# A delta-rule chunk chain on 64-row by 64-column quarters of the array, and a padded LoRA product

## The chip, the cores and the metric

The kernel runs on one core of one Trainium2 chip. A core has TensorE (PE, matmuls into PSUM banks), VectorE (DVE), ScalarE (ACT), GpSimdE (POOL) and SyncE (SP, which issues most DMAs). The metric is device time in microseconds of one execution; lower is better. The kernel before was run three times: 1617.15, 1622.96 and 1626.52 us, median 1622.96 us.

A matmul `mm(out, lhsT, rhs)` computes `lhsT.T @ rhs`. `lhsT` is loaded into the array as the stationary operand (the trace shows this as PEld), `rhs` is streamed through it. Slices of 64 partitions use 64 rows of the array, and the partitions of `out` decide which columns of the array are used. In the trace's rows "64\*64 64x64" means 64 rows by 64 columns of the array, and an output of 64 partitions by 64 elements. A float32 matmul stands in the trace as two records, a float32r matmul as one.

## The reference, cut to what matters

The block has differential attention and an RWKV-7 branch; both are merged, projected and followed by a feed-forward part. The change touches the RWKV-7 branch only:

```python
w = -jax.nn.softplus(-(w0 + jnp.tanh(wd) @ w2)) - 0.5     # LoRA of the decay
a = jax.nn.sigmoid(a0 + ad @ a2)                          # LoRA of a
def step(state, inp):                                     # 1024 steps, 8 heads of 64x64 state
    r_t, w_t, k_t, v_t, a_t, b_t = inp
    sa = jnp.einsum('bhvk,bhk->bhv', state, a_t)
    state = (state * w_t[:, :, None, :] + sa[..., None] * b_t[:, :, None, :]
             + v_t[..., None] * k_t[:, :, None, :])
    return state, jnp.einsum('bhvk,bhk->bhv', state, r_t)
```

Everything is computed in float32 accuracy: a float32 operand of a projection is split into a high and a low float32r part, and three of the four products are added (`mm3`).

## The kernel before, in words

**Stages.** `rwkv_parallel` projects the inputs and does all of the RWKV-7 branch that needs no state: for each pair of heads (4) and each 256 tokens (4) one `rwkv_unit`, with two calls of `lora_mm` (L395). These 32 calls stand between the projections' 128x512 matmuls, in an order that the scheduler chose. `lora_mm` makes two products of 256 columns: `lw2h` or `la2h`, the high weights, on 128 rows (the high part of x on partitions 0 to 63, its low part on 64 to 127), and `lw2l` or `la2l`, the low weights, on 64 rows, with the high part of x alone.

Then attention, the inversion of small triangular matrices, the gate projections (`gates`, L1059) and the state recurrence (`chain`, L917) run together. From there on TensorE's order is written out by hand: each part is a generator that yields the time from which its next piece can go on, and `drive` (L1488) takes the ready one of the lowest rank. The clock of this plan, `self.now`, is not the chip's: `mm` adds a fixed cost for each matmul (0.214 us for a float32 matmul with 128 stationary columns, 0.07 us with 64). So a cost in `mm` decides how many gate matmuls (`ps_d<-h_hi,whi` and its like) stand between two steps of the chain. After the chain, `branch_a` goes on with the same filling, then merge, output projection and feed-forward, all of 128x512 matmuls.

**The chain.** It has 16 chunks of 64 tokens, and in each the 8 heads as 4 pairs. A pair's two heads stand on partitions 0 to 63 and 64 to 127. `Sb` (state), `Ub` (corrections) and `Vb` (values) are block-diagonal, 128 x 4 x 128, with zeros off the diagonal, so that one 128x128 product handles both heads. One chunk takes three stretches of matmuls, with other work between:

1. `AK` @ `Vb` (4 products, 128 rows by 128 columns), `KT` @ `Vb` (8 products, 64 by 64, one for each head on the diagonal quarters), `AR` @ `Sb` (4 products, 128 by 128). ACT and DVE copy the upper half of the result to `R`.
2. `T` @ `R` (8 products, 64 by 64). ACT and DVE copy it to `Ub`.
3. `BT` @ `Ub` (8 products, 64 by 64), then `RB` @ `Ub` (4 products, 128 rows by 64 columns). DVE adds the first to `W` (the decayed state, from POOL) to give the next `Sb`; ACT copies the second to `yn`, from which the group norm starts.

Bank `g` holds AK, AR and RB; bank `us` holds T in one half and KT with BT in the other. After stretch 1 the chain yields for `LH1` (2.106 us), after 2 for `LH2` (1.8 us), after 3 for `LH` (2.215 us). In the trace the tile names `ps_r<-Vb,ch`, `ps_r<-Sb,ch`, `ps_r<-R,cT` and `ps_r<-Ub,ch` are AK with KT, AR, T, and BT with RB. In the first chunk there is no AR, in the last no KT and no BT.

Of the kernel before, what the change touches and what calls it, by code (L numbers as in the profile page):

```python
# [81 lines left out]
class Block:  # L82
# [102 lines left out]
    def mm(self, out, lhsT, rhs, **k):  # L185
        self.pe(self.nc.tensor.matmul(out, lhsT=lhsT, rhs=rhs, **k))  # L186
        if rhs.dtype == F32R:
            self.now += max(0.06, rhs.free_size() * 0.000417)
        else:
            self.now += {P: 0.214, C: 0.07}.get(lhsT.free_size(), 0.04)  # L190
# [165 lines left out]
    def loras(self):  # L356
# [7 lines left out]
        for src, nm in ((self.lw2, "lw2"), (self.la2, "la2")):  # L364
# [4 lines left out]
            lo = p.tile([C, HB], F32R, name=nm + "l")  # L369
            nc.scalar.copy(hi, raw)  # L370
            nc.vector.tensor_tensor(lo, raw[0:C], f32(hi[0:C]), ALU.subtract)
# [23 lines left out]
    def lora_mm(self, which, pr, u, tag):  # L395
# [7 lines left out]
        self.mm(ps, lhsT=wl[:, cs], rhs=x[0:C], start=False, stop=True)  # L403
# [513 lines left out]
    def chain(self):  # L917
# [7 lines left out]
        def zeroed(nm):  # L925
            t = p.tile([P, 4, P], F32, name=nm)
            nc.gpsimd.memset(t, 0.0)
            return t

# [5 lines left out]
        Sb, Ub, Vb = zeroed("Sb"), zeroed("Ub"), (zeroed("Vb0"), zeroed("Vb1"))  # L935
        lds = {}

        def load(c):
# [5 lines left out]
            for h in range(2):  # L944
                nc.sync.dma_start(Vb[c % 2][H[h], :, H[h]], self.d_vt[c, H[h]])
# [9 lines left out]
        for c in range(NC_):  # L955
# [3 lines left out]
            ld, Vc = lds.pop(c), Vb[c % 2]  # L959
            T = ld["T"]  # L960
            R = p.tile([P, 4, C], F32, tag="R", name="R")

            g = self.pst("r").rearrange("p (r x) -> p r x", x=P)
            us = self.pst("r").rearrange("p (z r x) -> p z r x", z=2, x=C)
            for pr in range(4):
                mm(g[:, pr, :], lhsT=ld["AK"][:, pr, :], rhs=Vc[:, pr, :], start=pr == 0, stop=False, skip_group_check=True)
            if not last:
                for pr in range(4):
                    for h in range(2):
                        mm(us[H[h], 1, pr, :], lhsT=ld["KT"][H[h], pr, :], rhs=Vc[H[h], pr, H[h]], start=pr == 0, stop=False, skip_group_check=True)  # L970
            if not first:
                for pr in range(4):
                    mm(g[:, pr, :], lhsT=ld["AR"][:, pr, :], rhs=Sb[:, pr, :], start=False, stop=False, skip_group_check=True)
            with self.hi_first():
                nc.scalar.copy(R[H[0]], g[H[0], :, H[0]])
                V.tensor_copy(R[H[1]], g[H[0], :, H[1]])
            yield self.now + LH1
            for pr in range(4):
                for h in range(2):
# [642 lines left out]
```

## Time and profile before

| what | value |
|---|---|
| median of three runs | 1622.96 us |
| the profiled execution's own time | 1619.49 us |
| its span, first to last instruction | 1617.7 us |
| PE busy | 1573.7 us, 97% of the span |
| DVE busy | 1114.6 us, 69% |
| ACT busy | 760.9 us, 47% |
| mean granted TensorE clock | 0.993 |

The busy time of PE is modelled and overlaps from one matmul to the next, so what a matmul costs is read as the time from its start to the start of the next one. In the rows of the timeline a group of equal matmuls has its first start and its count; the cost of a group is the next row's start less its own.

### The profile page before, as it was taken

Reading aid. Unit: us, or ns where it says so; the run is one execution under the profiler, and the core shown is the slowest. Engines: PE = TensorE matmul, PEld = TensorE weight load, DVE = VectorE, ACT = ScalarE, POOL = GpSimd, SP = SyncE. Lnnn points to the kernel's source line nnn. Section 1 sums busy time; section 2 is a strip of 40 time slices with the busy share of each in tenths; the row PEclk is TensorE's granted clock in tenths of the full one; section 3 lists DMA queues with packets and bytes.
Section 4 is the critical chain, followed back from the end, with each engine's and each line's share of the span. In section 5 each row is a group of like instructions: output and inputs, shape, how many; then the busy total and the mean of one; then the engine's idle time right before and its main releaser. Section 6 shows DMA issues by size and latency. Waiting matters only on the chain.

```text
span 1617.7 us, 24697 instructions
## 1 busy us (share of the span) xinstructions
PE 1573.7 (97%) x8786; PEld 1305.9 (81%) x8786; DVE 1114.6 (69%) x2201; ACT 760.9 (47%) x1509; POOL 141.6 (9%) x337
## 2 busy tenths in 40 slices
PE   9999999989999999999999999999999999999997
PEld 7888878868777887787877888888888888888887
DVE  7657677776596576767358678766676557977646
ACT  6533434443445554554334455444445454554423
POOL 2100000000011233323330000000000000000000
PEclk9999999999999999999999999999999999999999
DMA  5224445455769765563674553555555578554403
GB/s 185 92 69 148 136 138 145 143 157 173 237 207 254 213 190 174 176 193 119 232 244 144 201 180 133 195 170 177 193 171 171 180 237 282 170 157 137 137 27 105
DMA packets 217997, 274.63 MB, mean 170 GB/s; under 512 B 89617, under 2 KB 125586, under 8 KB 217618
## 3 DMA queue, kind: packets, MB, share of 16 engines
q1 hardware_dynamic: 208946, 251.46, 49.7%
q0 software_dynamic: 3456, 12.58, 2.5%
q10 hardware_dynamic: 5472, 9.02, 1.5%
q8 instruction: 69, 1.13, 0.3%
q14 instruction: 54, 0.44, 0.1%
HBM read 178.10 MB, written 94.90 MB: 169 GB/s over the span
## 4 chain that ended last, share of the span: by engine, by line
PE 84%; DVE 6%; DMA 6%; issue 1%; ACT 1%; POOL 1%; SPq 0%; ACTq 0%; DVEq 0%; POOLq 0%
PE ps_d L186 22%; PE ps_e L186 19%; PE ps_r L186 19%; PE ps_t L186 14%; PE ps_s L186 9%; PE ps_t L193 2%; DMA sin<-in_sin_dram 1%; DMA x_in<-in_xT_dram 1%; DMA q_s<-d_q 1%; DMA d_ch<-AR 1%; DMA bv<-d_bv 1%; DMA y_in<-d_yb 0%; DMA tb<-d_gt 0%; DVE sm L841 0%; DMA lraw<-in_la_dram 0%
## 5 line engine op out<-in xcount | busy, mean ns | idle before, releaser
L201 ACT CAST whi<-wraw 128x1024 fp32r<-128x1024 f32 (+1 forms) x122 | 114.1, 937 | 152.5 <-PE ps_d L186 53.6
L202 DVE TENSOR_TENSOR wlo<-wraw,whi 128x1024 fp32r<-128x1024 f32 (+1 forms) x122 | 133.5, 1094 | 37.3 <-ACT whi L201 37.0
L186 PE MATMUL ps_d<-h_hi,whi 128*128 128x512 f32 x344 | 141.5, 411 | 3.6 <-DVE rope L692 1.9
L186 PE MATMUL ps_d<-h_hi,wlo 128*128 128x512 f32 x344 | 137.5, 400 | 0.0
L186 PE MATMUL ps_d<-h_lo,whi 128*128 128x512 f32 x344 | 137.0, 398 | 0.1
L201 ACT CAST wop<-wop 128x512 fp32r<-128x512 f32 x98 | 60.9, 621 | 105.8 <-DMA wop<-d_z 103.4
L202 DVE TENSOR_TENSOR wop<-wop 128x512 fp32r<-128x512 f32 x98 | 67.3, 687 | 56.2 <-ACT wop L201 56.0
L186 PE MATMUL ps_e<-h_hi,whi 128*128 128x512 f32 x256 | 102.0, 398 | 0.0
L186 PE MATMUL ps_e<-h_hi,wlo 128*128 128x512 f32 x256 | 101.8, 398 | 0.0
L186 PE MATMUL ps_e<-h_lo,whi 128*128 128x512 f32 x256 | 101.0, 394 | 0.1
L186 PE MATMUL ps_r<-wop 128*128 128x512 f32 x294 | 86.0, 389 | 0.0
L186 PE MATMUL ps_s<-wop 128*128 128x512 f32 x294 | 85.8, 389 | 0.0
L186 PE MATMUL ps_t<-wop 128*128 128x512 f32 x294 | 85.8, 389 | 0.0
L186 PEld LDWEIGHTS ps_d<-h_hi,whi 128*128 128x128 f32 x344 | 65.5, 190 | 18.4 <-ACT gt L1072 2.3
L202 DVE TENSOR_TENSOR wop<-w,wop 128x512 fp32r<-128x512 f32 x98 | 67.0, 685 | 16.0 <-ACT wop L201 15.4
L186 PEld LDWEIGHTS ps_d<-h_hi,wlo 128*128 128x128 f32 x344 | 65.2, 190 | 14.5
L186 PEld LDWEIGHTS ps_d<-h_lo,whi 128*128 128x128 f32 x344 | 65.5, 190 | 11.8 <-DVE h_lo L290 0.5
L201 ACT CAST wop<-w 128x512 fp32r<-128x512 f32 x98 | 60.6, 619 | 17.4 <-DVE w L1363 8.9
L186 PEld LDWEIGHTS ps_t<-wop 128*128 128x128 f32 x294 | 55.2, 188 | 11.5
L186 PEld LDWEIGHTS ps_r<-wop 128*128 128x128 f32 x294 | 55.2, 188 | 11.5
L186 PEld LDWEIGHTS ps_s<-wop 128*128 128x128 f32 x294 | 55.2, 188 | 11.4
L866 POOL TENSOR_TENSOR p<-p 128x512 f32<-128x512 f32 (+3 forms) x32 | 35.9, 1121 | 255.8 <-ACT p L865 239.8
(469 smaller groups left out, 4093.5 us busy)
## 6 DMA issues: line engine op xcount, KB each, us to landing
wop<-d_z SPq DMA_DIRECT2D x98, 256.0 KB
wraw<-in_w_dram SPq DMA_DIRECT2D x32, 512.0 KB
w<-in_w_dram SPq DMA_DIRECT2D x64, 256.0 KB
ch<-d_ch SPq DMA_DIRECT2D x16, 896.0 KB
wraw<-in_win_dram POOLq DMA_DIRECT2D x24, 512.0 KB, 4.3
d_z<-t SPq DMA_DIRECT2D x42, 256.0 KB
wraw<-in_win_dram SPq DMA_DIRECT2D x18, 512.0 KB
d_gt<-gt ACTq DMA_DIRECT2D x32, 256.0 KB
```

The source lines that it names most:

```text
L186: self.pe(self.nc.tensor.matmul(out, lhsT=lhsT, rhs=rhs, **k))
L193: self.pe(self.nc.tensor.transpose(*a, **k))
L201: self.nc.scalar.copy(hi, src)
L202: self.nc.vector.tensor_tensor(lo, src, f32(hi), ALU.subtract)
L866: self.nc.gpsimd.tensor_tensor(p0, p0, p1, ALU.add)
```

## The change

In the chain no operand is block-diagonal any more. `Sb`, `Ub` and `Vb` are 128 x 4 x 64, without zeros, and every product is 64 rows by 64 columns. AK and AR become four products for each pair of heads, in the four quarters of the array (16 each, where there were 4), RB two for each pair (8 for 4). The heads of a pair write to different banks: bank h holds head h's AK, AR and RB in its first half. The T products of both heads are in the second half of bank 0, KT and BT in that of bank 1. KT moves from stretch 1 to the front of stretch 2. ACT copies all of `Ub`, DVE adds all of `Sb` in one instruction, POOL makes `W` in one instruction and is asked for it before stretch 3, and `yn` is copied half by ACT and half by DVE. `Vb` is loaded by one DMA for a chunk, not two, and the four memsets of zeros go. In `mm` a float32 product with 64 rows is given 0.045 us in the plan.

In `loras` the low weights get 64 rows of zeros below, by a memset on POOL, so that the second product of `lora_mm` is 128 rows too.

```diff
--- before.py
+++ after.py
@@ -186,6 +186,9 @@
         self.pe(self.nc.tensor.matmul(out, lhsT=lhsT, rhs=rhs, **k))
         if rhs.dtype == F32R:
             self.now += max(0.06, rhs.free_size() * 0.000417)
+        elif rhs.shape[0] == C:
+
+            self.now += 0.045
         else:
             self.now += {P: 0.214, C: 0.07}.get(lhsT.free_size(), 0.04)
 
@@ -366,9 +369,11 @@
             nc.sync.dma_start(raw[0:C], src)
             nc.sync.dma_start(raw[C:P], src)
             hi = p.tile([P, HB], F32R, name=nm + "h")
-            lo = p.tile([C, HB], F32R, name=nm + "l")
+
+            lo = p.tile([P, HB], F32R, name=nm + "l")
+            nc.gpsimd.memset(f32(lo[C:P]), 0.0)
             nc.scalar.copy(hi, raw)
-            nc.vector.tensor_tensor(lo, raw[0:C], f32(hi[0:C]), ALU.subtract)
+            nc.vector.tensor_tensor(lo[0:C], raw[0:C], f32(hi[0:C]), ALU.subtract)
             self.lw.append((hi, lo))
         self.lx = []
         for n in range(NH):
@@ -400,7 +405,7 @@
         ps = self.pst(tag)[:, 0:UT]
         cs = slice(pr * P, (pr + 1) * P)
         self.mm(ps, lhsT=wh[:, cs], rhs=x, start=True, stop=False)
-        self.mm(ps, lhsT=wl[:, cs], rhs=x[0:C], start=False, stop=True)
+        self.mm(ps, lhsT=wl[:, cs], rhs=x, start=False, stop=True)
         return ps
 
 
@@ -922,17 +927,14 @@
         mm = self.mm
         H = (slice(0, C), slice(C, P))
 
-        def zeroed(nm):
-            t = p.tile([P, 4, P], F32, name=nm)
-            nc.gpsimd.memset(t, 0.0)
-            return t
-
         self.g2h = p.tile([P, HB], F32R, name="g2h")
         self.g2l = p.tile([P, HB], F32R, name="g2l")
         raw = p.tile([P, HB], F32, tag="gnq", name="lraw")
         nc.sync.dma_start(raw, self.lg2)
         self.split(self.g2h, self.g2l, raw)
-        Sb, Ub, Vb = zeroed("Sb"), zeroed("Ub"), (zeroed("Vb0"), zeroed("Vb1"))
+
+        Sb = p.tile([P, 4, C], F32, name="Sb")
+        Ub = p.tile([P, 4, C], F32, name="Ub")
         lds = {}
 
         def load(c):
@@ -941,8 +943,8 @@
             nc.sync.dma_start(t, self.d_ch[c])
             for nm, o, x in (("AK", CH_AK, P), ("AR", CH_AR, P), ("KT", CH_KT, C), ("BT", CH_BT, C), ("RB", CH_RB, C)):
                 ld[nm] = t[:, :, o:o + x]
-            for h in range(2):
-                nc.sync.dma_start(Vb[c % 2][H[h], :, H[h]], self.d_vt[c, H[h]])
+            ld["V"] = p.tile([P, 4, C], F32, tag="Vb", name="Vb", bufs=2)
+            nc.sync.dma_start(ld["V"], self.d_vt[c])
             T = p.tile([P, 4, C], F32, tag="cT", name="cT", bufs=2)
             nc.sync.dma_start(T, self.d_tt[c].rearrange("r h s t -> (h s) r t"))
             ld["T"] = T
@@ -956,54 +958,57 @@
             first, last = c == 0, c == NC_ - 1
             if not last:
                 load(c + 1)
-            ld, Vc = lds.pop(c), Vb[c % 2]
-            T = ld["T"]
+            ld = lds.pop(c)
+            Vc, T = ld["V"], ld["T"]
             R = p.tile([P, 4, C], F32, tag="R", name="R")
 
-            g = self.pst("r").rearrange("p (r x) -> p r x", x=P)
-            us = self.pst("r").rearrange("p (z r x) -> p z r x", z=2, x=C)
-            for pr in range(4):
-                mm(g[:, pr, :], lhsT=ld["AK"][:, pr, :], rhs=Vc[:, pr, :], start=pr == 0, stop=False, skip_group_check=True)
-            if not last:
+
+
+            banks = [self.pst("r").rearrange("p (z r x) -> p z r x", z=2, x=C) for _ in range(2)]
+            g, us = [b[:, 0] for b in banks], [b[:, 1] for b in banks]
+
+            def pairs(f):
                 for pr in range(4):
                     for h in range(2):
-                        mm(us[H[h], 1, pr, :], lhsT=ld["KT"][H[h], pr, :], rhs=Vc[H[h], pr, H[h]], start=pr == 0, stop=False, skip_group_check=True)
+                        f(pr, h, H[h])
+
+            def quads(nm, x, start):
+                for pr in range(4):
+                    for h, z in ((0, 0), (1, 1), (0, 1), (1, 0)):
+                        mm(g[h][H[z], pr, :], lhsT=ld[nm][H[h], pr, H[z]], rhs=x[H[h], pr, :], start=start and pr == 0, stop=False, skip_group_check=True)
+
+            quads("AK", Vc, True)
             if not first:
-                for pr in range(4):
-                    mm(g[:, pr, :], lhsT=ld["AR"][:, pr, :], rhs=Sb[:, pr, :], start=False, stop=False, skip_group_check=True)
+                quads("AR", Sb, False)
             with self.hi_first():
-                nc.scalar.copy(R[H[0]], g[H[0], :, H[0]])
-                V.tensor_copy(R[H[1]], g[H[0], :, H[1]])
+                nc.scalar.copy(R[H[0]], g[0][H[0]])
+                V.tensor_copy(R[H[1]], g[1][H[0]])
             yield self.now + LH1
-            for pr in range(4):
-                for h in range(2):
-                    mm(us[H[h], 0, pr, :], lhsT=T[H[h], pr, :], rhs=R[H[h], pr, :], start=last and pr == 0, stop=True, skip_group_check=True)
+            if not last:
+                pairs(lambda pr, h, i: mm(us[1][i, pr, :], lhsT=ld["KT"][i, pr, :], rhs=Vc[i, pr, :], start=False, stop=False, skip_group_check=True))
+            pairs(lambda pr, h, i: mm(us[0][i, pr, :], lhsT=T[i, pr, :], rhs=R[i, pr, :], start=False, stop=True, skip_group_check=True))
             with self.hi_first():
-                nc.scalar.copy(Ub[H[0], :, H[0]], us[H[0], 0])
-                V.tensor_copy(Ub[H[1], :, H[1]], us[H[1], 0])
+                nc.scalar.copy(Ub, us[0])
+                if not (first or last):
+                    W = p.tile([P, 4, C], F32, tag="W", name="W")
+                    nc.gpsimd.tensor_tensor(W, Sb, self.eC[:, :, c:c + 1].broadcast_to([P, 4, C]), ALU.mult)
             yield self.now + LH2
             if not last:
-                for pr in range(4):
-                    for h in range(2):
-                        mm(us[H[h], 1, pr, :], lhsT=ld["BT"][H[h], pr, :], rhs=Ub[H[h], pr, H[h]], start=False, stop=True, skip_group_check=True)
+                pairs(lambda pr, h, i: mm(us[1][i, pr, :], lhsT=ld["BT"][i, pr, :], rhs=Ub[i, pr, :], start=False, stop=True, skip_group_check=True))
+            pairs(lambda pr, h, i: mm(g[h][H[1], pr, :], lhsT=ld["RB"][i, pr, :], rhs=Ub[i, pr, :], start=False, stop=True, skip_group_check=True))
+            if not last:
                 with self.hi_first():
                     if first:
-                        nc.scalar.copy(Sb[H[0], :, H[0]], us[H[0], 1])
-                        V.tensor_copy(Sb[H[1], :, H[1]], us[H[1], 1])
+                        V.tensor_copy(Sb, us[1])
                     else:
-                        W = p.tile([P, 4, C], F32, tag="W", name="W")
-                        for h in range(2):
-                            nc.gpsimd.tensor_tensor(W[H[h]], Sb[H[h], :, H[h]], self.eC[H[h], :, c:c + 1].broadcast_to([C, 4, C]), ALU.mult)
-                        for h in range(2):
-                            V.tensor_tensor(Sb[H[h], :, H[h]], us[H[h], 1], W[H[h]], ALU.add)
-            for pr in range(4):
-                mm(g[H[1], pr, :], lhsT=ld["RB"][:, pr, :], rhs=Ub[:, pr, :], start=False, stop=True, skip_group_check=True)
+                        V.tensor_tensor(Sb, us[1], W, ALU.add)
             if c % 2 == 0:
                 y = p.tile([P, 8, C], F32, tag="yn", name="yn", bufs=3)
                 yn.append(y)
-            row = slice((c % 2) * C, (c % 2) * C + C)
+            yv = y[(c % 2) * C:(c % 2) * C + C].rearrange("p (r h) v -> p h r v", h=2)
             with self.hi_first():
-                nc.scalar.copy(y[row].rearrange("p (r h) v -> p r (h v)", h=2), g[H[1]])
+                nc.scalar.copy(yv[:, 0], g[0][H[1]])
+                V.tensor_copy(yv[:, 1], g[1][H[1]])
             if c % 2 == 1:
                 self.group_norm(p, y)
             ready = self.now + LH
```

On PE, stretches 2 and 3 of the chain's second chunk: `R,cT` is T, `Ub,ch` is BT and RB, `ones,osq` belongs to attention, `h_hi,whi`, `h_lo,whi` and `h_hi,wlo` are the gates. Before:

```order
L186 MATMUL ps_d<-h_hi,wlo 128x512
L186 MATMUL ps_r<-R,cT 64x64 x8
L186 MATMUL ps_t<-ones,osq 128x1 x4
L186 MATMUL ps_d<-h_hi,whi 128x512
L186 MATMUL ps_d<-h_lo,whi 128x512
L186 MATMUL ps_d<-h_hi,wlo 128x512
L186 MATMUL ps_d<-h_hi,whi 128x512
L186 MATMUL ps_d<-h_lo,whi 128x512
L186 MATMUL ps_d<-h_hi,wlo 128x512
L186 MATMUL ps_r<-Ub,ch 64x64 x8
L186 MATMUL ps_r<-Ub,ch 64x128 x4
L186 MATMUL ps_d<-h_hi,whi 128x512
```

And now, at the same place:

```order
L186 MATMUL ps_d<-h_hi,wlo 128x512
L186 MATMUL ps_r<-Vb,ch 64x64 x8
L186 MATMUL ps_r<-R,cT 64x64 x8
L186 MATMUL ps_t<-ones,osq 128x1 x4
L186 MATMUL ps_d<-h_hi,whi 128x512
L186 MATMUL ps_d<-h_lo,whi 128x512
L186 MATMUL ps_d<-h_hi,wlo 128x512
L186 MATMUL ps_d<-h_hi,whi 128x512
L186 MATMUL ps_d<-h_lo,whi 128x512
L186 MATMUL ps_d<-h_hi,wlo 128x512
L186 MATMUL ps_r<-Ub,ch 64x64 x16
L186 MATMUL ps_d<-h_hi,whi 128x512
```

KT stands ahead of T, stretch 3 is of one shape, and the filling between is the same. A few rows of filling later on PE stands stretch 1 of the third chunk, before:

```order
L186 MATMUL ps_d<-h_hi,wlo 128x512
L186 MATMUL ps_r<-Vb_5533,ch 128x128 x4
L186 MATMUL ps_r<-Vb_5533,ch 64x64 x8
L186 MATMUL ps_r<-Sb,ch 128x128 x4
L186 MATMUL ps_t<-ident,tot 128x128 x4
```

and now:

```order
L186 MATMUL ps_d<-h_hi,wlo 128x512
L186 MATMUL ps_r<-Vb,ch 64x64 x16
L186 MATMUL ps_r<-Sb,ch 64x64 x16
L186 MATMUL ps_t<-ident,tot 128x128 x4
```

Stretch 1 went from three shapes to one, and from 16 matmuls to 32. Ahead of the chain nothing moved on PE: its first 2008 rows are the same. On DVE, at stretch 3 of the second chunk (`sm`, `ps_s`, `rr`, `wtl` are attention's), before:

```order
L839 MEMSET ps_s 64x64
L983 COPY Ub<-ps_r 64x4x64
L841 TENSOR_REDUCE sm<-ps_s 128x1
L839 MEMSET ps_e 64x64
L841 TENSOR_REDUCE sm<-ps_e 128x1
L998 TENSOR_TENSOR Sb<-ps_r,W 64x4x64 x2
L860 RECIPROCAL rr<-tot 128x1
```

and now:

```order
L844 MEMSET ps_s 64x64
L846 TENSOR_REDUCE sm<-ps_s 128x1
L844 MEMSET ps_e 64x64
L846 TENSOR_REDUCE sm<-ps_e 128x1
L865 RECIPROCAL rr<-tot 128x1
L866 TENSOR_SCALAR rr<-rr,tot,nlam 128x1
L1004 TENSOR_TENSOR Sb<-ps_r,W 128x256
L1011 COPY yn<-ps_r 64x4x64
```

The copy to `Ub` left DVE, `Sb` is one instruction for two, and half of `yn` came.

## Rows read from the trace of the kernel before

**Rows 1.** The page: busy us of each engine (share of the span) xinstructions.

```profile
PE 1573.7 (97%) x8786; PEld 1305.9 (81%) x8786; DVE 1114.6 (69%) x2201; ACT 760.9 (47%) x1509; POOL 141.6 (9%) x337
```

**Rows 2.** By stretch: us, busy of PE, PEld, DVE, ACT, POOL; clock, DMA, GB/s.

```profile
60.00:420.00 360.00, 352.10 (x1741) 287.99 (x1740) 250.81 (x548) 151.79 (x365) 10.02 (x19) 0.99 0.48 138
545.00:790.00 245.00, 230.68 (x1985) 194.38 (x1984) 163.67 (x445) 121.76 (x305) 75.28 (x209) 0.99 0.59 178
790.00:1600.00 810.00, 807.79 (x3662) 669.65 (x3661) 559.98 (x866) 388.06 (x631) 24.45 (x26) 1.00 0.53 174
```

**Rows 3.** PE's longest waits, 545 to 790: us in total, times, longest.

```profile
PE ps_e L186 <- ACT p L850: 3.3, 2, 1.7
PE ps_r L186 <- DVE Ub L983: 2.2, 3, 1.7
```

**Rows 4.** Timeline of PE, one chunk: start, us, what, xcount [idle <-releaser].

```profile
653.27 0.39 PE L186 MATMUL ps_d<-h_hi,wlo 128*128 128x512 f32 x1
653.59 0.68 PE L186 MATMUL ps_r<-R,cT 64*64 64x64 f32 x16
654.20 0.50 PE L186 MATMUL ps_d<-h_hi,whi 128*128 128x512 f32 x1
654.53 0.39 PE L186 MATMUL ps_d<-h_lo,whi 128*128 128x512 f32 x1
...
656.47 1.70 PE L186 MATMUL ps_r<-Ub,ch 64*64 64x64 f32 x24
658.09 0.50 PE L186 MATMUL ps_d<-h_hi,whi 128*128 128x512 f32 x1
...
661.13 1.67 PE L186 MATMUL ps_r<-Vb,ch 128*128 128x128 f32 x24
662.73 1.16 PE L186 MATMUL ps_r<-Sb,ch 128*128 128x128 f32 x8
663.65 0.71 PE L186 MATMUL ps_s<-k_in,q_s 128*128 128x512 f32 x2
```

**Rows 5.** Timeline of PE, two cuts inside the 16 records of T.

```profile
653.69 0.57 PE L186 MATMUL ps_r<-R,cT 64*64 64x64 f32 x14
...
654.04 0.23 PE L186 MATMUL ps_r<-R,cT 64*64 64x64 f32 x2
```

**Rows 6.** Timeline of PE, products of 32 by 32 in the inversion.

```profile
513.87 1.20 PE L186 MATMUL ps_t<-yt,T 32*32 32x32 f32 x64
515.00 0.33 PE L186 MATMUL ps_s<-k_in,q_s 128*128 128x128 f32 x1
```

**Rows 7.** Timeline of PE, the last chunk: AK and AR without KT.

```profile
775.31 1.05 PE L186 MATMUL ps_r<-Vb,ch 128*128 128x128 f32 x8
...
777.09 0.28 PE L186 MATMUL ps_t<-ident,tot 128*128 128x128 f32 x1
```

**Rows 8.** Timeline of PE, one `lora_mm`; and a 256-column product among its like.

```profile
330.60 0.40 PE L186 MATMUL ps_d<-h_lo,whi 128*128 128x512 f32 x1
330.84 0.28 PE L186 MATMUL ps_r<-sa,la2h 128*128 128x256 f32 x1
331.05 0.39 PE L186 MATMUL ps_r<-sa,la2l 64*128 64x256 f32 x1
331.36 0.50 PE L186 MATMUL ps_d<-h_hi,wlo 128*128 128x512 f32 x1
331.70 0.40 PE L186 MATMUL ps_d<-h_hi,whi 128*128 128x512 f32 x1
...
647.23 0.28 PE L186 MATMUL ps_t<-wth,v_in 128*128 128x256 f32 x1
647.35 0.28 PE L186 MATMUL ps_t<-wtl,v_in 128*128 128x256 f32 x1
```

**Rows 9.** A group of DVE, 545 to 790: count, busy us, mean ns, idle.

```profile
L983 DVE COPY Ub<-ps_r 64x256 f32<-64x256 f32 x16 | 6.8, 428 | 4.2 <-ACT Ub L982 3.8
```

**Rows 10.** Timeline of POOL, the first arithmetic after start-up, with the idle before it.

```profile
27.30 0.20 POOL L250 TENSOR_TENSOR newton<-rcol 128x4 f32<-128x4 f32 x1 [17.12 <-DVE lsm L732]
```

## The prediction

> **What bounds the kernel now.** The page's busy times come first: PE 97% of the span, the next engine 69% [rows 1]. The reader should then ask whether that holds where the change is. The table by stretch says so: in the LoRA stretch (60 to 420 us) PE works for 352.1 of 360 us, in the chain's (545 to 790 us) for 230.7 of 245, and from 790 to 1600 us for 807.8 of 810 [rows 2]. So PE waits for 7.9 and 14.3 us in the two stretches that change, and hardly at all behind them: what comes late there would not be caught up, and what PE saves there comes off the end. The table of waits shows who PE waits for in the chain's stretch: attention's softmax first (3.3 us), then the copy to `Ub` (2.2 us) [rows 3]. There is no one long wait to remove; the change has to be priced as PE time. For that the timeline of PE is read, start to start, since busy times overlap.
>
> **The unit: a step.** T has 16 records, two for each product, and heads of a pair lie on diagonal quarters of the array. From the third record to the fifteenth it takes 654.04 - 653.69 = 0.35 us [rows 5]: six pairs of records, 0.058 us for a pair. A full 128 by 128 record with 128 columns costs 1.78 / 16 = 0.111 us [rows 7]. Half the columns, half the time, and two records go at once. I call 0.058 us a step. T as a whole lies between the starts at 653.59 and 654.20, 0.61 us, of which 8 steps are 0.47 and 0.14 is left; the matmul ahead takes 653.59 - 653.27 = 0.32, the one behind 654.53 - 654.20 = 0.33 [rows 4], where its like takes 0.24 (330.60 to 330.84) [rows 8]. So going into 64 by 64 and out again costs 0.14 + 0.08 + 0.09 = 0.31 us each time.
>
> **The chain, part by part.** Before, a middle chunk costs: stretch 1 from 661.13 to 663.65, 2.52 us; T 0.61 + 0.17 = 0.78; BT and RB from 656.47 to 658.09, 1.62 + 0.17 = 1.79 [rows 4]. Together 5.09 us.
>
> Now every stretch is of one shape. AK and AR are 32 products, 64 records, on four quarters. The trace of before shows no product in two quarters of the same rows at once, so the price has two bounds: four records to a step (16 steps, 0.93 us), if the quarters work side by side as the diagonal ones do, or two to a step (32 steps, 1.86 us), if a row of quarters takes one product at a time. I take the first: the 32 by 32 products show that records can follow each other at 1.13 / 64 = 0.018 us with entry and exit in it [rows 6], against the 0.0145 that four to a step need, so issuing is hardly in the way; and the step went with the columns of one tile (0.111 for 128, 0.058 for 64), not with the records. KT with T is 16 steps of pairs, as measured, 0.93 us. BT is 8 steps, RB is 16 records whose heads have different rows and different banks but the same columns: 8 steps side by side, or 16 one by one. Side by side again, for the same reason. So each stretch is 0.93 + 0.31 = 1.24 us, a chunk 3.72, and 5.09 - 3.72 = 1.37 is saved in each of 14 middle chunks: 19.2 us. The first has no AR: before, 2.52 less the 0.92 from 662.73 to 663.65, with T and stretch 3, 4.17; now 0.78 + 1.24 + 1.24 = 3.26; 0.9 saved. The last has neither KT nor BT: before 1.78 [rows 7] + 0.78 + 1.18 = 3.74; now 1.24 + 0.78 + 0.78 = 2.80; 0.9 saved. **The chain's sum is 21.0 us.**
>
> **The padded LoRA product.** The 64-row product stands between 128-row ones. The `la2h` ahead takes 331.05 - 330.84 = 0.21, `la2l` 0.31, the 512-column one behind it 331.70 - 331.36 = 0.34 [rows 8]: 0.86 us. Among its like a 256-column product takes 0.12 and a 512-column one 0.24 [rows 8], so with no change of shape 0.48. That is 0.38 for each of 32 calls: **12.2 us**. Its lower bound is nothing, if these products only fill time in which PE would wait; the 7.9 us of waits in 360 speak against that. The zeros cost two memsets on POOL, ahead of its first arithmetic, for which POOL had been idle for 17.12 us [rows 10]. What is behind them on POOL is the constants and then the weight loads and Newton steps; I cost them at nothing while that gap stands, and at their own length on the first projections if it were gone.
>
> **What else moves.** On DVE the copy to `Ub` (428 ns, 16 times [rows 9]) goes, `Sb` is one instruction for two, and a copy of half of `yn` comes, of about the length of that to `Ub`. ACT and POOL have less to do. None of them bounds, so this counts for nothing in the sum, except that the wait for DVE's `Ub` (2.2 us) can end earlier. SP issues 15 or 16 fewer loads. One wait is new: both banks are now read at the end of a chunk by DVE, `Sb` and then `yn`, so the next chunk's AK waits for DVE's copy of `yn`, where it waited for ACT's. Behind AK stands all of PE's queue. The filling between RB's end and AK is 661.13 - 658.09 = 3.04 us [rows 4], against a copy of 0.43 us behind one addition of about the same length; I cost it at nothing with that cover, and see below for the case without it. KT in front of T waits for the same copies to `R` as T did, and puts 0.47 us between them and `Ub`; the filling behind covers it.
>
> **The sum.** 21.0 + 12.2 = 33.2 us less on PE. Not all of it will reach the end: the other engines' chains in these stretches do not get shorter by as much, and PE will meet some of them earlier. I take an eighth off (an estimate: a little over the 22.2 us of waits in 605 us that stand there now, since the work removed is all PE's): 29 us. Against the profiled execution's own 1619.5 us that is **1590 us**; the median of the runs shown is 3.5 us above that execution, which I leave to the range. The granted clock is 0.99 in both stretches [rows 2] and counted as it is.
>
> **The rivals.**
> *Quarters in pairs.* A row of quarters takes one product at a time. Stretch 1 is then 1.86 + 0.31 = 2.17 us, a middle chunk 4.65, 0.44 saved; first chunk 0.5, last none: 6.7 us in all, or, if RB's heads take turns too (8 more steps, 0.46 us, 16 times), 0.7 less than nothing. With the LoRA part and an eighth off: 1603, to 1610. For it: nothing in the trace shows more than two at once. Against it: the step's length follows the columns. A floor on the pace of records would do the same. The Trainium skill (TensorE: Matmul & The Clock Gate, section "Wait — 56ns, not 53.3ns?") says that start to start never drops below about 25 ns, however small the product; by that stretch 1 would be 0.67 us longer and the result about 1599. The 0.018 us of the 32 by 32 products [rows 6] are below that floor, so the trace does not agree.
> *A load that waits for its neighbour: slower.* Stationary and streamed columns overlap now: a step of 64 and 64 is no longer than either. If a quarter's load had to wait for the matmul in the other quarter of its rows, load and stream would follow each other, 0.116 us for a pair. Stretch 1 then takes 32 x 0.116 + 0.31 = 4.0 us, a middle chunk 6.5, 1.4 lost in each: 20 us, with the first (0.4) and last (1.8) 22 us. Less 10.7 from LoRA this ends 11 us slower, at 1631. The place is stretch 1 alone, and it decides from about 44 ns for one of its 992 records in all chunks, three times the forecast's. Against it: the same quarter is loaded anew every step in T, and that load overlaps. A rule of the Trainium skill speaks for it (TensorE: Matmul & The Clock Gate, section "The mechanism", under "What overlaps and what doesn't"): a load overlaps running matmuls only when its row group differs. T's 0.058 us for a pair, loaded into the rows that are at work, does not fit the rule as it stands [rows 5].
> *The new wait.* If DVE is late with `yn` by 1 us in each of 15 chunks, half the gain goes: about 1605.
> *The padding gives nothing.* PE then waits where it worked: 21.0 less an eighth, 1601.
>
> **How the numbers follow.** Forecast 0.64 (1581 to 1598: nothing lost, or a quarter lost, and 4 us of what one execution differs from another); pairs 0.18 (1599 to 1610); the new wait 0.06 (1598 to 1610); no gain from padding 0.06 (1597 to 1603); slower 0.06 (1625 to 1640). The range, 1581 to 1608, leaves out the slower case, most of the turns of RB and the forecast's tails. A measurement of this kernel can tell about 0.5% from no change, 8 us. Faster by more: forecast, padding, most of pairs and of the new wait, 0.87; within it 0.07; slower 0.06.
>
> **What would show it.** In the profile after: stretch 1 (`Vb,ch` with `Sb,ch`) near 1.1 us from its start to the next start says four at a time, near 2.0 pairs, near 3.9 the load that waits. `Ub,ch` near 1.1 us says that RB's heads run side by side. `la2l` on 128 rows at 0.12 us, with 0.24 for the one behind, shows the padding. The idle of PE before `ps_r<-Vb,ch`, ended by DVE, is the new wait; none over 0.3 us is forecast. The forecast is wrong if these are as said and PE's waits in the two stretches grow from 22 us by over 10.

## The result, and the profile after

The changed kernel takes 1602.49 us (median), the kernel before 1620.06 us beside it: ratio 0.9898, 95% interval 0.9872 to 0.9925. Timed once more in the experiments below, it takes 1599.62 against 1619.21 us, ratio 0.9884 (0.9863 to 0.9904). That is 17 to 20 us less, where 33 were saved on paper and 29 forecast. The profiled execution takes 1602.98 us. On its page PE is as full as before [rows 1]:

```profile
PE 1546.8 (97%) x9658; PEld 1287.8 (80%) x9658; DVE 1103.9 (69%) x2187; ACT 756.2 (47%) x1508; POOL 131.6 (8%) x321
```

By stretch (length, then busy time of PE, PEld, DVE, ACT, POOL; clock, DMA, GB/s), in answer to [rows 2]:

```profile
60.00:420.00 360.00, 348.11 (x1775) 292.19 (x1774) 254.22 (x556) 155.52 (x371) 10.07 (x19) 0.99 0.50 142
545.00:790.00 245.00, 223.54 (x2921) 184.70 (x2920) 159.35 (x431) 121.99 (x312) 76.55 (x210) 0.99 0.61 190
790.00:1590.00 800.00, 796.40 (x3633) 661.43 (x3632) 557.56 (x881) 385.39 (x628) 13.80 (x10) 1.00 0.53 171
```

PE now waits for 11.9 us of 360 and 21.5 of 245, where it waited for 7.9 and 14.3: 11.2 us more. Each part of the change is as short as priced all the same. PE's timeline through one chunk, in answer to [rows 4] (start, modelled length, records; the cost is the next row's start less its own):

```profile
641.94 0.40 PE L186 MATMUL ps_d<-h_hi,wlo 128*128 128x512 f32 x1
642.27 0.69 PE L186 MATMUL ps_r<-Vb,ch 64*64 64x64 f32 x32
642.78 0.65 PE L186 MATMUL ps_r<-Sb,ch 64*64 64x64 f32 x32
643.36 0.50 PE L186 MATMUL ps_d<-h_hi,whi 128*128 128x512 f32 x1
643.70 0.40 PE L186 MATMUL ps_d<-h_lo,whi 128*128 128x512 f32 x1
...
648.23 0.68 PE L186 MATMUL ps_r<-Vb,ch 64*64 64x64 f32 x16
648.74 0.63 PE L186 MATMUL ps_r<-R,cT 64*64 64x64 f32 x16
649.31 0.50 PE L186 MATMUL ps_d<-h_hi,whi 128*128 128x512 f32 x1
...
651.81 1.15 PE L186 MATMUL ps_r<-Ub,ch 64*64 64x64 f32 x32
652.89 0.50 PE L186 MATMUL ps_d<-h_hi,whi 128*128 128x512 f32 x1
```

AK takes 0.51 us for 32 records, as long as KT with 16 (648.23 to 648.74): four quarters work at once. The stretches are 643.36 - 642.27 = 1.09, 1.08 and 1.08 us, together 3.25, against 2.52 + 0.61 + 1.62 = 4.75 [rows 4]: 1.50 less in each of 14 middle chunks. Summed over all records of the chain, start to start, it is 21.5 us less. The matmuls right beside the chain's take 2.3 us more in all, since stretch 1, once of its neighbours' shape, now has a way in and out as well. The forecast's 21.0 had that counted, so it is to be held against 19.2.

One LoRA call, in answer to [rows 8]: the two products and the matmul behind them take 0.12 + 0.13 + 0.24 = 0.49 us for 0.86. Over the calls it is 0.39 us each, 12.4 us in all, for 12.2 forecast.

```profile
342.73 0.28 PE L186 MATMUL ps_r<-sw,lw2h 128*128 128x256 f32 x1
342.85 0.28 PE L186 MATMUL ps_r<-sw,lw2l 128*128 128x256 f32 x1
342.98 0.40 PE L186 MATMUL ps_e<-h_hi,wlo 128*128 128x512 f32 x1
343.22 0.39 PE L186 MATMUL ps_e<-h_hi,whi 128*128 128x512 f32 x1
```

So the prices held, and some 40% of the 19.2 + 12.4 = 31.6 us that they save did not arrive. Who PE waits for in the chain's stretch (545 to 790 us; us in total, times, longest), in answer to [rows 3]:

```profile
PE ps_d L186 <- ACT gt L1077: 3.2, 2, 1.6
PE ps_s L186 <- ACT p L855: 3.0, 3, 1.4
PE ps_t L196 <- ACT osq L896: 2.7, 2, 1.5
PE ps_e L186 <- ACT p L855: 2.7, 2, 2.2
PE ps_t L186 <- POOL tot L256: 2.3, 1, 2.3
```

The wait for DVE's `Ub` is gone, and none for `yn` came. In its place are many waits for attention's softmax and its norm, and for the gates' `gt`. From the first score product to the merge, the stretch in which attention and chain run, is 433.4 us before and 422.9 after. Its two ends, before and after:

```profile
458.44 0.33 PE L186 MATMUL ps_s<-k_in,q_s 128*128 128x128 f32 x2
...
891.88 0.39 PE L186 MATMUL ps_d<-m_hi,whi 128*128 128x512 f32 x1
```

```profile
452.19 0.33 PE L186 MATMUL ps_s<-k_in,q_s 128*128 128x128 f32 x2
...
875.07 0.40 PE L186 MATMUL ps_d<-m_hi,whi 128*128 128x512 f32 x1
```

I call it the attention stretch. It is 10.6 us shorter, where the chain gives 19.2. The other 8.6 us are in two things that overlap in part. PE's idle time, summed over every pause of more than 0.15 us, is 27.0 us here and was 20.1. And 13.7 us of the stretch are at 1.2 GHz, where it was 6.8; at most half of such time is lost.

### The profile page after: what moved, and what is told of

It is laid out like the page before. It is cut to its first block, busy times and chain, and to the rows that moved or that the text cites. A ratio compares the mean times of both kernels' runs of the same rounds, so it can differ in the third digit from the quotient of the medians.

```text
span 1601.2 us, 26387 instructions
## 1 busy us (share of the span) xinstructions
PE 1546.8 (97%) x9658; PEld 1287.8 (80%) x9658; DVE 1103.9 (69%) x2187; ACT 756.2 (47%) x1508; POOL 131.6 (8%) x321
## 4 chain that ended last, share of the span: by engine, by line
PE 78%; DVE 9%; DMA 6%; ACT 2%; issue 2%; POOL 1%; SPq 0%; ACTq 0%; DVEq 0%; POOLq 0%
PE ps_d L186 21%; PE ps_e L186 18%; PE ps_r L186 16%; PE ps_t L186 14%; PE ps_s L186 9%; PE ps_t L196 1%; DMA bv<-d_bv 1%; ACT p L855 1%; DVE sm L846 1%; DMA x_in<-in_xT_dram 1%; DMA y_in<-d_ya 1%; DMA sin<-in_sin_dram 1%; DMA d_ch<-AR 1%; DVE itmp L629 0%; DMA d_q<-qhi 0%
## 5 line engine op out<-in xcount | busy, mean ns | idle before, releaser
L205 DVE TENSOR_TENSOR wlo<-wraw,whi 128x1024 fp32r<-128x1024 f32 (+1 forms) x122 | 131.9, 1081 | 31.4 <-ACT whi L204 31.1
L186 PE MATMUL ps_d<-h_hi,whi 128*128 128x512 f32 x352 | 145.0, 412 | 5.0 <-ACT gt L1077 3.2
L186 PE MATMUL ps_d<-h_lo,whi 128*128 128x512 f32 x352 | 140.8, 400 | 0.0
L186 PE MATMUL ps_e<-h_hi,whi 128*128 128x512 f32 x248 | 98.0, 395 | 0.0
L186 PE MATMUL ps_e<-h_hi,wlo 128*128 128x512 f32 x248 | 97.7, 394 | 0.0
L186 PE MATMUL ps_e<-h_lo,whi 128*128 128x512 f32 x248 | 97.1, 391 | 0.0
L186 PEld LDWEIGHTS ps_d<-h_hi,whi 128*128 128x128 f32 x352 | 67.3, 191 | 18.1 <-ACT gt L1077 3.7
```

The costliest lines, as they stand in the source:

```text
L205: self.nc.vector.tensor_tensor(lo, src, f32(hi), ALU.subtract)
```

## Experiments

Each kernel was timed beside the kernel before; ratios are to that. Because one execution differs from another by some us, the traces are read by the length of a stretch too: the LoRA stretch from the first `la2l` to the last, and the attention stretch. PE's idle time is counted as above; the expectations count PE's waits some us higher.

**First theory: what PE saves is given back wherever it then meets a load or a chain of ACT and DVE.** In the profiled execution the last `la2l` starts only 5.9 us earlier than before, and DVE waits there for the load of the rotary table `sin`. The first pair of runs takes the two parts of the change alone.

*The padding alone*, in the kernel before:

```diff
-            lo = p.tile([C, HB], F32R, name=nm + "l")
+            lo = p.tile([P, HB], F32R, name=nm + "l")
+            nc.gpsimd.memset(f32(lo[C:P]), 0.0)
...
-        self.mm(ps, lhsT=wl[:, cs], rhs=x[0:C], start=False, stop=True)
+        self.mm(ps, lhsT=wl[:, cs], rhs=x, start=False, stop=True)
```

> The kernel before with LoRA's low weights padded and nothing else. Theory (PE's saved time is given back wherever PE then waits for a load or a chain of ACT and DVE that ends at its own time): every one of the 32 LoRA calls is shorter by 0.39 us as in the changed kernel, 12.4 us in all, but only about half of it is left where the last call ends (near 417 us before), and the kernel is 5 to 7 us faster (ratio 0.9957 to 0.9969). Rival 1 (the unit price arrives whole): 12 us faster, ratio 0.9926. Rival 2 (the padding gives nothing and the whole gain is the chain's): ratio 1.000 within 0.001.

Measured: 1609.56 against 1617.22 us, ratio 0.9946 (0.9928 to 0.9965), 8.7 us less.

*The chain alone*, the changed kernel with these lines turned back:

```diff
-            lo = p.tile([P, HB], F32R, name=nm + "l")
-            nc.gpsimd.memset(f32(lo[C:P]), 0.0)
+            lo = p.tile([C, HB], F32R, name=nm + "l")
...
-        self.mm(ps, lhsT=wl[:, cs], rhs=x, start=False, stop=True)
+        self.mm(ps, lhsT=wl[:, cs], rhs=x[0:C], start=False, stop=True)
```

> The changed kernel with LoRA's low weights unpadded, 64 rows as before: the chunk chain's part alone. Theory: the bodies of the chain's stretches are as in the changed kernel (1.09, 1.08 and 1.08 us, 1.4 to 1.5 us less per middle chunk, some 21 us in all), of which 6 to 8 us go into longer waits of PE for the softmax of the attention that runs beside it, so 9 to 14 us faster (ratio 0.9914 to 0.9944). Rival (the two parts hinder each other, each alone would arrive whole): 20 us faster, ratio 0.988, the same as both together.

Measured: 1610.89 us, ratio 0.9968 (0.9946 to 0.9991), 5.2 us less; the attention stretch is 423.7 us long, its chain records 21.6 us less than before. The padding alone leaves the attention stretch at 431.3 us. The parts add up to 13.9 us, against 17 to 20 for both. The intervals of the parts (3 to 4 us to either side of each) allow that, so there is no sign that they hinder each other. The padding brings most of its price, the chain a quarter to a half.

How much of the padding arrives is told by the LoRA stretch (group of `la2l`: shortest, median and longest in ns, first and last start). Before, in the changed kernel, and with the padding alone:

```profile
L186 PE MATMUL ps_r<-sa,la2l x16: 379/380/573, 61.5 to 416.9; 64*128 64x256 f32 x16
```

```profile
L186 PE MATMUL ps_r<-sa,la2l x16: 276/282/363, 61.5 to 411.0; 128*128 128x256 f32 x16
```

```profile
L186 PE MATMUL ps_r<-sa,la2l x16: 276/282/365, 61.2 to 402.3; 128*128 128x256 f32 x16
```

The last two have the same order on PE up to the chain, yet 349.5 and 341.1 us. Over all kernels with before's order or the padded order on PE there, four traces without padding have 352.4 to 355.4 us (mean 353.9), eight with it 341.1 to 349.5 (mean 344.1): 9.8 of 12.4 us arrive. The profiled execution was at the long end, and the half that seemed lost in it was mostly that.

*Two buffers for the tables* was meant to take the wait for `sin` away, in the changed kernel and, as a control, in the kernel before:

```diff
-                cn = p.tile([P, HB], F32, tag="cos", name="cos")
-                sn = p.tile([P, HB], F32, tag="sin", name="sin")
+                cn = p.tile([P, HB], F32, tag="cos", name="cos", bufs=2)
+                sn = p.tile([P, HB], F32, tag="sin", name="sin", bufs=2)
...
```

Three small tiles elsewhere share the buffers of others to make room.

> The changed kernel with two buffers each for the tiles cos and sin of the rotary tables (four small tiles elsewhere share a buffer to make room), so that a table's load can be issued one use earlier. Theory (a part of LoRA's gain was given back at VectorE's wait for the load of sin, 7.3 us at 222 to 232 us and 6.6 us near 310): these waits, 17.9 us of VectorE in 60 to 420 us, fall below 5 us, PE's idle time at the transposes of zv that hangs on them falls by 3 to 5 us, the last LoRA call ends 3 to 6 us earlier than in the changed kernel, and the time is 1596 to 1600 us (ratio to the kernel before 0.985 to 0.988). Rival (the load hides behind other work, or the next wait ends just as late): the waits of VectorE go, but the last LoRA call ends within 1 us of where it did, and the ratio stays 0.990.

> The kernel before with the same two buffers each for cos and sin. Theory: the waits for sin (15.5 us of VectorE in 60 to 420 us) fall here as well, but PE, slower by 0.39 us a call, waited less on them: 1 to 4 us faster (ratio 0.9975 to 0.9994), less than the same edit gives the changed kernel. Rival (the wait is as dear in the kernel before, so it took nothing of the change's gain): the same gain as in the changed kernel, within 1 us.

Measured: 0.9945 (0.9926 to 0.9964) and 1.0009 (0.9994 to 1.0024), no gain in either, and a loss for the changed kernel. The edit did not do what it was for: DVE still waits 17.0 us for `sin` (17.9 in the changed kernel), since one load and its multiplication moved ahead of 60 us and the others wait as they did. It tells nothing on that wait; the LoRA stretch, 346.8 us, is among the others. The loss is in the attention stretch, 428.9 us, whose order moved too.

**Second theory: the waits stand behind the group norm in DVE's order.** One of the two longest waits of the changed kernel's attention stretch, 2.15 us, read backwards (all engines; the other, of 2.3 us, is for POOL's `tot`):

```profile
571.48 0.42 DVE L985 COPY R<-ps_r 64x256 f32<-64x256 f32 x1
571.93 0.75 DVE L914 SCALAR_TENSOR_TENSOR osq<-o,vecs,ps_t 128x512 f32<-128x512 f32 x1
...
574.89 0.69 DVE L1032 TENSOR_TENSOR yn<-yn,gn 128x512 f32<-128x512 f32 x1 [2.22 <-POOL gn L256]
...
575.50 0.68 DVE L846 TENSOR_REDUCE sm<-ps_e 128x1 f32<-128x512 f32 x1
...
577.51 0.69 ACT L855 ACTIVATE p<-ps_e,sm 128x512 f32<-128x512 f32 x1 [3.53 <-DVE ps_s L849]
...
578.34 0.73 PE L186 MATMUL ps_e<-k_in,q_s 128*128 128x512 f32 x2 [2.15 <-ACT p L855]
```

PE needs bank `ps_e`, which ACT frees with the exponential, for which DVE first has to find the maximum `sm`, in two parts (L846 and, two instructions later, L849, which is what ACT's row names). DVE stands still for 2.22 us at the last multiplication of the group norm, since POOL's Newton steps are not done, and the maximum is next in its order. In the kernel before, the maximum comes before that multiplication, and nothing waits:

```profile
577.61 0.42 DVE L976 COPY R<-ps_r 64x256 f32<-64x256 f32 x1 [0.79 <-ACT R L975]
578.11 0.75 DVE L909 SCALAR_TENSOR_TENSOR osq<-o,vecs,ps_t 128x512 f32<-128x512 f32 x1
578.77 0.69 DVE L841 TENSOR_REDUCE sm<-ps_e 128x1 f32<-128x512 f32 x1
...
581.66 0.43 DVE L983 COPY Ub<-ps_r 64x256 f32<-64x256 f32 x1
582.12 0.69 DVE L1027 TENSOR_TENSOR yn<-yn,gn 128x512 f32<-128x512 f32 x1
```

From the copy of `R` to the maximum it is 1.16 us before and 4.02 after. Over 545 to 790 us DVE's wait for POOL there is, before and after:

```profile
DVE yn L1027 <- POOL gn L253: 2.5, 2, 1.7
```

```profile
DVE yn L1032 <- POOL gn L256: 13.0, 7, 3.7
```

That window leaves out the last of these waits of the kernel before. Over the whole attention stretch it is 6.0 us in 3 waits before, against 13.0 in 7. The other way round, DVE's wait for PE's scores at the maximum falls there from 6.2 us to 1.1: DVE is now the one that comes late.

What moved here is DVE's order, which the scheduler makes; the hand-written order holds PE alone. Such a wait can cost a second time. Behind this one the granted clock is at 1.2 GHz (0.50) for a while, and a matmul that elsewhere takes 0.24 us (342.98 to 343.22 above) takes 0.43 (580.84 to 581.27):

```profile
580.20:583.00 2.80, 2.80 (x9) 2.17 (x8) 2.24 (x7) 1.73 (x5) 1.90 (x2) 0.50 0.55 174
```

```profile
580.84 0.63 PE L186 MATMUL ps_d<-h_lo,whi 128*128 128x512 f32 x1
581.27 0.63 PE L186 MATMUL ps_d<-h_hi,wlo 128*128 128x512 f32 x1
```

Two edits were tried, beside the changed kernel itself, whose trace gives 423.0 us for the attention stretch, much as the first:

> The changed kernel itself, timed in more rounds beside the experiments. All theories: ratio 0.989 to 0.990. If the two parts add up as in their runs alone (8.7 and 5.2 us by the ratios), it is 0.9914; if the first timing holds, 0.9898. In its trace: the chain's own records 21 to 22 us less than before between the first score product and the merge, PE's waits in the same stretch 8 to 9 us more.

*The Newton steps on DVE.*

```diff
-        self.rsqrt(s[:, 16:24], s[:, 24:32], nc.gpsimd)
+        self.rsqrt(s[:, 16:24], s[:, 24:32])
```

> The changed kernel with the Newton steps of the group norm on VectorE (9 instructions each time) in place of GpSimd (12). Theory (VectorE, freed of half the copies, now comes to the last multiply of the group norm before GpSimd has ended the Newton steps, and the softmax behind it in VectorE's order, on which PE waits, stands still: 9.5 us in 6 waits in the changed kernel against 2.5 in 2 before): these waits are gone, VectorE's work grows by 8 times some 1.5 us, PE's longest wait at the second score product (2.3 us near 576 us) is under 1 us, PE's waits between the first score product and the merge fall from 30 us by 2 to 5, and the time falls by as much: ratio to the kernel before 0.986 to 0.988. Rival (VectorE's extra work stands ahead of the softmax as long as the wait did): PE's waits within 1.5 us of the changed kernel's, ratio within 0.001 of it.

> The kernel before with the same edit of the group norm. Theory: there the wait for GpSimd is 2.5 us in all, so the edit trades it for more of VectorE's work and gives nothing: ratio 0.999 to 1.001. Rival (GpSimd's Newton steps cost the kernel before as much): 2 to 5 us faster, ratio 0.997 to 0.999, and the wait took nothing of the change's gain.

Measured: 0.9889 (0.9863 to 0.9915) in the changed kernel, no gain; 1.0012 (0.9995 to 1.0028) in the kernel before. DVE's wait for POOL is gone, and for the time the rival holds: the steps stand where the wait stood. PE's idle time, 31.1 us, and the attention stretch, 426.8 us, are above those of the changed kernel, which neither theory nor rival expected. DVE's timeline at the same place:

```profile
564.28 0.42 DVE L985 COPY R<-ps_r 64x256 f32<-64x256 f32 x1
...
565.94 0.69 DVE L1032 TENSOR_TENSOR yn<-yn,gn 128x512 f32<-128x512 f32 x1
566.55 0.74 DVE L914 SCALAR_TENSOR_TENSOR osq<-o,vecs,ps_t 128x512 f32<-128x512 f32 x1
567.21 0.68 DVE L846 TENSOR_REDUCE sm<-ps_e 128x1 f32<-128x512 f32 x1
```

From `R` to the maximum it is still 2.93 us. So POOL's slowness by itself is not the cause. PE's order is that of the changed kernel here.

*No group norm at all*, in the changed kernel and in the kernel before:

```diff
-                self.group_norm(p, y)
+                pass
```

> The changed kernel with the chain's group norm left out (y goes on without it): VectorE loses 8 times some 4 us of work and all waits for GpSimd's Newton steps there, ScalarE 8 squares of 0.63 us. Theory (PE's added waits are the softmax's instructions standing in VectorE's order behind the group norm): PE's waits between the first score product and the merge fall from 29.5 us by 5 or more, and the time by 5 to 9 us, ratio 0.983 to 0.986. Rival (the softmax waits for its own chain of product, maximum, exponential, and the order on PE asks for it too early): waits within 2 us, time within 2 us of the changed kernel, ratio 0.987 to 0.990.

> The kernel before with the chain's group norm left out (y goes on without it), the control to the same edit of the changed kernel, where it took some 10 us. Theory (the change made the softmax stand behind the group norm on VectorE, which it hardly did before: VectorE waited 2.5 us for the Newton steps before, 9.5 after): 1 to 5 us faster, ratio 0.997 to 0.9995, PE's waits between the first score product and the merge between 17 and 21.4 us. Rival (the group norm costs PE as much in the kernel before, so it took nothing of the change's gain): 8 to 12 us faster, ratio 0.9925 to 0.995, waits down by 6 us or more.

Measured: 0.9807 (0.9773 to 0.9840) in the changed kernel, some 12 us below it; 0.9980 (0.9960 to 0.9999) in the kernel before, 3 us below. The attention stretch is 411.6 us (from 422.9) and 428.1 (from 433.4), PE's idle time in it 18.1 us (from 27.0) and 15.4 (from 20.1). The place of the 2.15 us wait, without group norm, has none (572.36 against 571.90), and the granted clock there is 1.00 (571 to 576 us):

```profile
567.79 0.71 PE L186 MATMUL ps_e<-k_in,q_s 128*128 128x512 f32 x2
...
571.90 0.62 PE L186 MATMUL ps_s<-k_in,q_s 128*128 128x512 f32 x2
572.36 0.62 PE L186 MATMUL ps_e<-k_in,q_s 128*128 128x512 f32 x2
```

PE's order is the same with the group norm and without, in both kernels (apart from which of some 32 by 32 products, which run side by side, starts first). So the group norm costs PE 3 to 5 us in the kernel before and 11 to 12 after: of the 8.6 us that the attention stretch gave back, 6 us by the lengths of the stretch ((422.9 - 411.6) - (433.4 - 428.1)), or 9 us by the ratios, whose intervals leave 2 to 16. The second theory holds for this much. Leaving it out also takes DVE's work away, so it doesn't show that the order alone would bring the 6 us.

**Is a microsecond of PE worth only half in this stretch?** If so, taking out more would again give half.

```diff
-                quads("AR", Sb, False)
+                pass
```

> The changed kernel with the products AR (the old state into the scores, 16 of the 32 of the first stretch) left out, so the state reaches neither U nor y; loads, copies and all else stay. It measures what a microsecond of PE's chain work is worth in this stage. PE's chain records fall by 15 times 0.577 = 8.7 us more. Theory (about half of what PE saves here goes into longer waits for VectorE and ScalarE): 3 to 6 us faster than the changed kernel, ratio to the kernel before 0.985 to 0.987, PE's waits between the first score product and the merge up by 3 to 5 us. Rival (the change's loss was a one-off of its order, PE's time counts whole): 8 to 9 us faster, ratio 0.983 to 0.984, waits within 2 us.

Measured: 0.9826 (0.9790 to 0.9862), 7 to 9 us below the changed kernel; the chain's records are 8.4 us less, the attention stretch 10.7 us (412.2), PE's idle time 23.5 us. This fits the rival: PE's time counts whole, and what the change lost is not a rate but what this one order of the engines cost. It does not prove it. The plan is shorter without these products, so the filling on PE between the chain's steps is ordered anew, and a new order alone can be worth as much, as the next runs say.

**Does the plan's price matter?** The change plans 0.045 us for each 64-row product; the trace says 1.09 / 32 = 0.034 for one of AK or AR and 1.08 / 16 = 0.068 for the others, without the way in and out. The run uses 0.036 for AK and AR (`self.quad`) and 0.0725.

```diff
-            self.now += 0.045
+            self.now += 0.036 if self.quad else 0.0725
...
```

> The changed kernel with the measured prices in the planner: a product of the first stretch 0.036 us, one of the two others 0.0725 us, where the change plans 0.045 for each; planned time of a middle chunk 3.5 us in place of 2.9. Theory (the order on PE is planned for stretches shorter than they are, so the softmax's results are asked for too early or too late): PE's waits between the first score product and the merge fall from 30 us by 2 to 6, ratio 0.986 to 0.988. Rival (the plan's prices hardly matter beside the latencies of VectorE and ScalarE, since a product asked for early waits for its engine in either order): waits within 2 us, ratio within 0.0015 of the changed kernel's.

Measured: 1595.23 us, ratio 0.9853 (0.9827 to 0.9878), the fastest complete kernel here, some 5 us below the changed one; the two intervals overlap. PE's idle time falls from 27.0 us (28.4 in the second trace) to 22.7, as the theory said. But 27.3 us of the attention stretch are at 1.2 GHz in this trace, against 13.7 and 10.2, and the stretch, 423.9 us, is no shorter. So the trace does not show where the 5 us are, and the theory's reason for them is shown only in part. With longer planned latencies besides:

```diff
-LB = 1.25
+LB = 1.6
-LCM = 0.426
+LCM = 0.55
-LW = 1.272
+LW = 1.6
```

> The changed kernel with the measured prices in the planner and, besides, the three planned latencies of the softmax a quarter longer (1.25 to 1.6, 0.426 to 0.55, 1.272 to 1.6 us). Theory (PE asks for the softmax's results too early since the chain between them has become shorter, and there is other work to put between): PE's waits in the stretch fall from 29.7 us in the kernel with prices alone by 3 or more, and the time is 2 to 5 us below it, ratio 0.982 to 0.984. Rival (the other work is used up, or VectorE's order moves the results as far back): waits within 2 us, ratio 0.984 to 0.988.

Measured: 0.9927 (0.9898 to 0.9956), 12 us slower than with the prices alone, against theory and rival. The attention stretch is 429.0 us, PE's idle time 31.9. PE's longest waits there are new ones:

```profile
PE ps_t L187 <- POOL tot L257: 6.2, 2, 6.0
PE ps_e L187 <- DMA y_in<-d_ya: 3.5, 2, 2.0
```

Both kernels do the same work on PE, so the order of this stretch can be worth 12 us, more than half of what the change brings.

## Why the prediction was right or wrong

**What bounds.** Right: PE's own time, before and after (a cut of 8.4 us of products gave 7 to 11).

**The unit prices.** Right to a few per cent: four records to a step, as forecast from the 32 by 32 products and T (stretch 1 at 1.09 us, forecast about 1.1); RB's heads side by side (1.08); in and out 0.10 and 0.11 us beside the stretch; 0.39 us for a LoRA call. The chain's 21.0 us measured 19.2 (21.5 in its own records, less 2.3 beside them), LoRA's 12.2 measured 12.4.

**What else moves.** No wait of PE for `yn` came, and that for `Ub` went, as said. "None of them bounds, so this counts for nothing in the sum" is the step that failed. DVE, 65% busy, bounds nothing, but its order changed around the copies that the change moved, and in that order the group norm held up the softmax: it costs PE 11 to 12 us in the changed kernel and 3 to 5 in the kernel before. The working looked at who waits for the copies, not at what else stands in DVE's queue with them.

**The sum.** An eighth off, 4 us, for what PE would meet earlier was too little: 2.6 us went in the LoRA stretch, 8.6 in the attention stretch. That is the mis-sized term. Its working gave no ground for it either: 22.2 us of waits in 605 is 3.7%, so an eighth is not a little over it but three times as much, and the share that was lost is about a third. The prediction's own mark against 1590 (prices as said, waits up from 22 us by over 10) is passed in the profiled execution, with 11.2 us more, and just missed in the second trace of the same kernel, with 8.5. The range reaches to 1608 for rivals that did not happen; that it holds the time is luck.

**The rivals.** None of them happened, though some give the right time. Quarters in pairs (1603) would show stretch 1 at 2.0 us, padding that gives nothing (1601) would show no gain for it alone, where 8.7 us were measured. A floor on the pace of records (1599) falls as well: AK's records follow each other at 0.51 / 32 = 0.016 us. That does not agree with the floor of about 25 ns from start to start in the Trainium skill (TensorE: Matmul & The Clock Gate, section "Wait — 56ns, not 53.3ns?"). The slower case, 1631, falls too: 64 records with a load each, in quarters that share their rows, take 1.09 us and not 3.9, so loads overlap matmuls in the same rows. That does not agree with the rule of the Trainium skill (the same page, section "The mechanism") as the prediction read it. The new wait (1605) did not come, as said. A time that fits a rival says nothing without the row that the rival names.

**What is open.** Where the rest of the chain's loss is: of 8.6 us, about 6 come with the group norm, and up to 3 with half clock, partly the same ones. By run, span times one less the mean granted clock is 14.3 to 16.3 us before (means of the four batches of runs), 15.7 with the padding, 18.9 with the chain alone and 18.2 with both: an estimate of what the 1.2 GHz stretches cost, some 3 us more with the chain's change, which the first profile (0.993 before, 0.988 after) already hints at. By the same measure 4 of the 12 us that the longer latencies lost are clock (23.7 us, against 19.4 with the prices alone). And why the plan's prices help.

## What to carry to other kernels

Price a change of PE's work by start-to-start times of its own rows and of the ones beside them: such prices held here. Then look at each engine whose instructions the change moves, idle or not, for what stands behind them in its order: a softmax behind a group norm on DVE cost about a third of what the chain saved. Compare such stretches over several traces, since two executions of one order differ by 8 us in 345 here, and let a control on the kernel before say whether the cost is the change's own.

## What was not expected of the hardware

Four 64 by 64 float32 products, with a load each, run in the four quarters of the array at once: 32 records in 0.51 us, the same as 16 on two diagonal quarters. A 128-row product in place of one with 64 rows between others of 128 is 0.39 us cheaper with its neighbours, although half of what it multiplies is zero. And a wait of PE of 2.15 us was followed by 2.8 us and more at 1.2 GHz (580.2 to 583), in which PE was busy all the time.
